# DeltaNet layer: modulation bias on VectorE and later in a round, scores on swapped PSUM banks, a later pause before the inverse's first block product

## The chip, the cores and the metric

The kernel runs on one core of a Trainium2 chip. The metric is the device time of one execution in microseconds (us). Before the change it was run three times: 2856.79 us (the median), 2857.01 and 2852.32 us. The profiled execution, from which all rows below come, took 2853.54 us, and its span is 2851.8 us.

## The reference, cut to what matters

The program is a trunk of two layers on a sequence of 1024 tokens with 1024 channels. Layer 0 mixes with a gated DeltaNet, layer 1 with stick-breaking attention, and each mixer is followed by a SwiGLU feed-forward part. Every sub-layer has a norm whose shift, scale and gate are modulations: six vectors of 1024 per layer, computed as `silu(c) @ ada_w + ada_b`. The change lies in the DeltaNet layer, which covers roughly the first 700 us:

```
G = cumsum(g);  decay = exp(G_i - G_j) where i >= j               # chunks of 64 tokens
A = where(i > j, (beta*k) k^T * decay, 0)                         # strictly lower, 64x64
U = solve(I + A, beta*v);   W = solve(I + A, beta*k*exp(G))       # the "inverse"
attn = q k^T * decay                                              # needs the scores q k^T
S' = S*exp(G_last) + k_tail^T (U - W S);  o = q_dec S + attn (U - W S)   # scan over 16 chunks
out = (rms_norm(o) * silu(z)) @ w_out                             # z: the gate's projection
```

There are 8 heads of dimension 128; the kernel takes one head per round.

## The kernel before, in words

`deltanet()` is a software pipeline over heads. In round t (`for t in range(-2, NH - 1)`, line 1246) five Python generators are merged: `stage_d(t-1)` (gates a finished head: the transposes L1235), `stage_c(t)` (the scan over chunks L1188 to L1203, and at its end the matmuls of the gate's projection z), `stage_b(t+1)` (scores, inverse, W and U of the next head), `stage_a(t+2)` (projections, convolution and norms of the head after that) and three or four modulations. After the merge, `logs()` runs the logarithms and exponentials of the norms (L977 to L991), for which ScalarE loads two tables.

`merge` (line 75) is a planner by a virtual time: each generator has a clock, starts at a head value from a list (`hd`), and each `yield x` moves its clock on by x; the one with the lowest clock issues next. The framework then schedules the instructions of each engine in one fixed order from these priorities, and inserts the semaphore waits. So a number at a `yield` or a head changes where instructions stand in all engines' queues, not how long a thing takes.

Matmul results go to PSUM banks of three pools: `big()` (tile name g, the large projections), `bank()` (name m, a ring of two banks) and `bank2()` (name s, a ring of two). `bank_swap()` takes them in turn by a counter that all its callers share: s on odd counts, m on even ones. A bank is free again when its reader, on ScalarE or VectorE, is done.

The names that the prediction uses:
- The scores are two groups of 128x64 matmuls per round, issued through `together` (whose matmuls carry the helper's lines L101 and L97), evicted by L1036 and its neighbours. The ax product (128x64 stationary, 64 moving columns) comes next.
- The inverse of I + A is made in steps. VectorE solves 16x16 blocks (L1062, L1064: `pr`, `X`), L1067 copies on ScalarE, L1069 transposes, L1072 writes the operands `dd`. Then come the block products of 32 matmuls of 64x64 each: **dd0** = `blocks(ao, d2[:, 0])` with the copy L1094, then three iterations in the loop behind it: **dd1**, **it1** and **it2**, evicted by L1100 (dd1, it1) and L1104 (it2, in two halves). Then a copy by identity (**ident**, L1112), L1108, a product S,S (L1116), a product S (L1124), and the W and U matmuls **L1133/L1137**.
- L887 transposes q, k and v of the next head, four at a time, evicted by the copies L888 on ScalarE.
- The gate: ScalarE's tanh L1148 reads all of the z projection, VectorE's L1149 multiplies. L898 and L899 are the same pair for the convolved projection.
- A modulation by rows is 8 matmuls of 32 stationary columns on an `ada` tile (`mod_rows`), a copy L200 to `adac`, one matmul L205 against a vector, and the bias addition L207.
- "gemm" below is a 128x512 matmul of a projection (L269, L271, L273; each weight is split into a high part by L263 on ScalarE and a low part by L264 on VectorE).

Of the kernel before, what the change touches and what calls it, by code (L numbers as in the profile page):

```python
# [12 lines left out]
AF = mybir.ActivationFunctionType  # L13
# [5 lines left out]
P = 128  # L19
# [12 lines left out]
def tile_trunk(ctx: ExitStack, tc: tile.TileContext, x_in, c_in, ada_w, ada_b, n1g, n2g, dn_w, dn_ab,  # L32
# [3 lines left out]
    V, S, G, PE, SY = nc.vector, nc.scalar, nc.gpsimd, nc.tensor, nc.sync  # L36
# [12 lines left out]
    def nm(s):  # L49
        uid[0] += 1  # L50
        return f"{s}_{uid[0]}"
# [7 lines left out]
    def bank(shape=(P, HALF)):  # L59
        return pm.tile(list(shape), F32, tag="m", name=nm("m"))  # L60

    def bank2(shape=(P, HALF)):
        return pq.tile(list(shape), F32, tag="s", name=nm("s"))
# [7 lines left out]
    def bank_swap(shape=(P, HALF)):  # L71
        alt[0] += 1
        return bank2(shape) if alt[0] % 2 else bank(shape)

    def merge(gens, totals=None, heads=None):

        live = [[heads[i] if heads else 0.0, i, g] for i, g in enumerate(gens)]
        rate = [1.0 / t for t in totals] if totals else [1.0] * len(gens)
        while live:
            live.sort(key=lambda e: (e[0], e[1]))  # L80
            e = live[0]
            try:
                e[0] += next(e[2]) * rate[e[1]]
            except StopIteration:
                live.remove(e)
# [5 lines left out]
    def together(made):  # L91

        last = None
        for n, f in enumerate(made):
            if n:
                with tc.high_priority():
                    ins = f()  # L97
                tc.add_manual_dep(ins.ins, last.ins.name, mybir.DependencyInfo(
                    mybir.DependencyClass.NoSync, mybir.DependencyReason.DATA), reason="together")
            else:  # L100
                ins = f()  # L101
            last = ins
# [5 lines left out]
    def const(name, shape, dt=F32):  # L108
        return cp.tile(list(shape), dt, tag=name, name=name)
# [28 lines left out]
    adab = scz[:, KT:].rearrange("p (a b) -> p a b", a=2)  # L138
# [15 lines left out]
    mod = const("mod", (P, 2, 48))  # L154

    def mod_add(ps, layer, j):
        V.tensor_tensor(out=mod[:, layer, j:j + 1], in0=ps, in1=adab[:, layer, j:j + 1], op=ALU.add)
# [45 lines left out]
    def mod_end(layer, j, acc, rows=False):  # L203
        ps = bank()
        PE.matmul(ps[:, 0:1], lhsT=acc, rhs=pick if rows else one1, start=True, stop=True)  # L205
        if rows:
            S.activation(out=mod[:, layer, j:j + 1], in_=ps[:, 0:1], func=AF.Identity, bias=adab[:, layer, j:j + 1])  # L207
        else:
            mod_add(ps[:, 0:1], layer, j)

    def first_mods(layer, q):

# [18 lines left out]
    def mod_steps(layer, js, aside=True, spare=False):  # L231
        last = None
        for j in js:
            acc = mod_unit(layer, j, aside, spare)
            if last:
                mod_end(layer, *last)
            last = (j, acc)
            yield 15.0
        mod_end(layer, *last)

    def row_steps(layer, js):
        for j in js:
            acc = mod_rows(layer, j)
            yield 15.0
            mod_end(layer, j, acc, True)
# [443 lines left out]
    def deltanet(h, after, there, second):  # L689
# [283 lines left out]
        def logs():  # L973

            pin = tc.keep_in_program_order if 1 else (lambda x: x)
            for rc, ln, bs, ot, rs in open_c:
                pin(S.activation(out=rc, in_=rc, func=AF.Ln, scale=1.0 / (P * P), bias=eps1))  # L977
            for hh, ln in open_a:
                pin(S.activation(out=ln[:, 0:2, :], in_=ln[:, 0:2, :], func=AF.Ln, bias=eps1))
            for rc, ln, bs, ot, rs in open_c:  # L980
                pin(S.activation(out=rc, in_=rc, func=AF.Exp, scale=-0.5))
                V.tensor_tensor(out=rc, in0=rc, in1=ln[:, 4, bs], op=ALU.mult)
                V.tensor_tensor(out=ot[:, bs], in0=ot[:, bs], in1=rs[:, bs].to_broadcast((P, bs.stop - bs.start, P)),
                                op=ALU.mult)
            for hh, ln in open_a:
                pin(S.activation(out=ln[:, 2:4, :], in_=ln[:, 0:2, :], func=AF.Exp, scale=-1.0))
                S.activation(out=ln[:, 4, :], in_=ln[:, 0, :], func=AF.Exp, scale=-0.5)
                S.activation(out=ln[:, 5, :], in_=ln[:, 1, :], func=AF.Exp, scale=0.5)
                V.tensor_tensor(out=ln[:, 6, :], in0=tpair[:, hh, :], in1=ln[:, 3, :], op=ALU.mult)
                V.tensor_tensor(out=ln[0:64, 8, :], in0=side[0:64, hh, :], in1=ln[0:64, 3, :], op=ALU.mult)  # L990
                V.tensor_tensor(out=ln[:, 7, :], in0=bcol[:, hh, :], in1=ln[:, 5, :], op=ALU.mult)  # L991
            open_a.clear()
            open_c.clear()

        def stage_b(hh):
# [30 lines left out]
            H = [slice(0, 64), slice(64, 128)]  # L1026
            qn = qk.rearrange("p a (n t) -> p a n t", t=P)
            for b in range(2):
                ps = bank((P, 4, 2, 64))
                together([partial(PE.matmul, ps[H[p], n, :, :], lhsT=qn[:, 1, 4 * b + n, H[p]],  # L1030
                                  rhs=qn[:, :, 4 * b + n, H[p]], start=True, stop=True)
                          for n in range(4) for p in range(2)])
                bs = slice(4 * b, 4 * b + 4)
                V.tensor_tensor(out=a1[:, bs], in0=ps[:, :, 1, :], in1=e[:, 1, bs], op=ALU.mult)
                for p in range(2):
                    V.tensor_tensor(out=at[H[p], bs, H[p]], in0=ps[H[p], :, 0, :], in1=e[H[p], 0, bs], op=ALU.mult)  # L1036
                yield 1.2

            ps = bank(C8)
# [40 lines left out]
            rg = slot("X2", (P, 2, KT, P))  # L1080
            rt, tg = rg[:, 0], rg[:, 1]
            cur0 = tg.rearrange("p n t -> p (n t)")[:, 0:KT * 64].rearrange("p (n t) -> p n t", t=64)
            yield 2.88

            def blocks(lt, rh, to=(0, 1)):

                ps = bank(C8)
                together([partial(PE.matmul, ps[H[o], n, :], lhsT=lt[H[p], n, :], rhs=rh[H[p], n, :], start=True, stop=True)
                          for n in range(KT) for p, o in (to if isinstance(to[0], tuple) else [(p, p) for p in to])])
                return ps  # L1090

            ps = blocks(ao, d2[:, 0])
# [4 lines left out]
            for it in range(3):  # L1097
                ps = blocks(nt, cur)
# [10 lines left out]
            ps = bank(C8)  # L1109
# [3 lines left out]
            ps = bank(C8)  # L1113
# [7 lines left out]
            ps = bank(C8)  # L1121
# [7 lines left out]
            for b in range(2):  # L1129
                bs = slice(4 * b, 4 * b + 4)  # L1130
                ps = bank2((P, 4, P))
# [3 lines left out]
                ps = bank((P, 4, P))  # L1135
# [32 lines left out]
        def gate_last():  # L1168
            last.append(big())
            yield 10.0  # L1170
            yield from gate_gemm(NH - 1, last[0])
# [68 lines left out]
        def stage_d(hh):  # L1240
            ot, sz = st_c.pop(hh)
            yield 3.6
            for b in range(2):
                turn_gate(ot, sz, b)
                yield 0.9
            SY.dma_start(out=yd[hh], in_=sz)

        mg = row_steps(0, range(16, 48))
        for t in range(-2, NH - 1):
            gens, hd = [], []  # L1250

            def add(g, k):
                gens.append(g)
                hd.append({'oC': 0.111, 'oM': 0.202}.get(k, 0.0))

            if t >= 1:
                add(stage_d(t - 1), 'oD')
            if t >= 0:
                add(stage_c(t), 'oC')
            if 0 <= t + 1:  # L1260
                add(stage_b(t + 1), 'oB')
            if t == -2:
                add(decays(), 'oX')
            if t + 2 < NH:
                add(stage_a(t + 2), 'oA')
            else:
                add(gate_last(), 'oA')
            add(islice(mg, (3, 3, 4, 4, 4, 4, 4, 3, 3)[t + 2]), 'oM')
            merge(gens, None, hd)
            logs()  # L1270
# [310 lines left out]
    rows = []  # L1581
# [100 lines left out]
```

## Time and profile before

| | |
|---|---|
| median of three runs | 2856.79 us |
| profiled execution, own time | 2853.54 us |
| its span | 2851.8 us |
| TensorE (PE) busy | 2726.1 us (96%) |
| VectorE (DVE) busy | 2019.9 us (71%) |
| ScalarE (ACT) busy | 1384.8 us (49%) |
| chain that ended last | PE 74%, DVE 11%, ACT 8%, DMA 3% |

A busy TensorE covers a matmul from its issue to its modelled end, so that the durations of neighbours overlap; how fast the engine works through a list is read from the starts. Idle time in brackets is the time in which an engine had nothing to run just before an instruction, with the instruction whose end released it. DeltaNet's rounds repeat: dd0 starts at 153.43, 220.43, 294.52, 371.43, 448.37, 525.22, 602.10 and 668.15 us, and L1137 at 175.71, 242.65, 319.85, 396.75, 473.69, 550.50, 628.18 and 688.10 us.

### The profile page before, as it was taken

What the parts mean: (1) busy time and instruction counts of PE and PEld (TensorE: products, weight loads), DVE (VectorE), ACT (ScalarE), POOL (GpSimd) and SP (SyncE); (2) the same over time, 40 slices, a digit from 0 to 9 for tenths busy, and PEclk for the clock granted to TensorE, in tenths of its full rate; (3) what the DMA queues carried; (4) which work ended last, traced back from release to release, by engine and by line L of the source; (5) the groups of instructions that cost most, each with busy time, mean ns of one, the idle gap of its engine ahead of it and who ended that gap; (6) DMA issues with size and microseconds to landing.
All of it is one profiled execution on the core that took longest, in us unless ns stands there. A gap on an engine that the chain in (4) does not pass through costs nothing.

```text
span 2851.8 us, 40133 instructions
## 1 busy us (share of the span) xinstructions
PE 2726.1 (96%) x15122; PEld 2171.4 (76%) x15122; DVE 2019.9 (71%) x3319; ACT 1384.8 (49%) x2924; POOL 132.8 (5%) x238
## 2 busy tenths in 40 slices
PE   6899999998999999999989999999899999999999
PEld 3677777777778887888877677677577888888887
DVE  5777666666597667667786777777868876667666
ACT  5545555554463334343245777777846332223222
POOL 0000000001000111111000000000000000000000
PEclk8999999998999999999999999999899999999999
DMA  6312222234222222222231111111412211111122
GB/s 228 106 54 82 79 72 80 72 107 133 71 85 66 68 82 71 81 75 78 67 118 52 53 52 52 53 53 50 139 52 93 61 54 57 48 56 48 56 59 100
DMA packets 139169, 218.41 MB, mean 77 GB/s; under 512 B 34016, under 2 KB 62560, under 8 KB 138976
## 3 DMA queue, kind: packets, MB, share of 16 engines
q1 hardware_dynamic: 138976, 215.86, 23.9%
q8 instruction: 119, 1.95, 0.3%
q14 instruction: 74, 0.61, 0.1%
HBM read 199.95 MB, written 15.86 MB: 76 GB/s over the span
## 4 chain that ended last, share of the span: by engine, by line
PE 74%; DVE 11%; ACT 8%; DMA 3%; issue 2%; POOL 1%; SPq 0%; ACTq 0%; POOLq 0%; DVEq 0%
PE m L269 10%; PE m L273 9%; PE m L271 9%; PE g L273 6%; PE g L269 6%; PE s L269 6%; PE s L273 6%; PE g L271 6%; PE s L271 6%; DVE S L1476 2%; PE m L97 2%; DMA ada<-in_ada_w_dram 1%; PE s L1489 1%; PE s L97 1%; PE m L101 1%
## 5 line engine op out<-in xcount | busy, mean ns | idle before, releaser
L269 PE MATMUL m<-h,wh 128*128 128x512 f32 x872 | 351.3, 411 | 12.1 <-ACT h L361 8.0
L269 PE MATMUL g<-h,wh 128*128 128x512 f32 x920 | 337.3, 405 | 10.9 <-ACT wh L263 5.8
L273 PE MATMUL m<-h,wl 128*128 128x512 f32 x872 | 341.4, 401 | 2.3 <-DVE wl L264 2.3
L273 PE MATMUL g<-h,wl 128*128 128x512 f32 x920 | 333.2, 400 | 9.1 <-DVE wl L264 9.0
L271 PE MATMUL m<-h,wh 128*128 128x512 f32 x872 | 341.1, 400 | 0.1
L271 PE MATMUL g<-h,wh 128*128 128x512 f32 x920 | 328.0, 397 | 0.0
L374 DVE SCALAR_TENSOR_TENSOR X<-m,mod,X 128x512 f32<-128x512 f32 x224 | 166.7, 749 | 202.0 <-PE m L273 201.6
L263 ACT CAST wh<-ga 128x512 fp32r<-128x512 f32 x160 | 95.7, 621 | 285.7 <-PE s L271 148.2
L273 PEld LDWEIGHTS g<-h,wl 128*128 128x128 f32 x920 | 171.9, 189 | 50.1 <-DVE wl L264 15.0
L269 PEld LDWEIGHTS m<-h,wh 128*128 128x128 f32 x872 | 167.6, 193 | 54.9 <-ACT h L361 9.8
L269 PEld LDWEIGHTS g<-h,wh 128*128 128x128 f32 x920 | 169.4, 190 | 49.1 <-ACT wh L263 10.5
L263 ACT CAST wh<-wr 128x512 fp32r<-128x512 f32 x202 | 124.7, 622 | 153.9 <-PE m L271 75.5
L271 PEld LDWEIGHTS g<-h,wh 128*128 128x128 f32 x920 | 172.1, 190 | 35.1 <-DVE h L349 0.5
L273 PEld LDWEIGHTS m<-h,wl 128*128 128x128 f32 x872 | 168.2, 193 | 39.6 <-DVE wl L264 3.1
L271 PEld LDWEIGHTS m<-h,wh 128*128 128x128 f32 x872 | 167.8, 192 | 32.9 <-DVE h L362 1.8
L1476 DVE TENSOR_TENSOR_SCAN S<-S,late 128x256 f32<-128x256 f32 (+7 forms) x128 | 171.4, 1358 | 24.3 <-ACT S L1471 24.3
L264 DVE TENSOR_TENSOR wl<-wr,wh 128x512 fp32r<-128x512 f32 x202 | 137.2, 684 | 42.0 <-ACT wh L263 41.9
L1471 ACT ACTIVATE S<-g,rq 128x512 f32<-128x512 f32 (+5 forms) x258 | 140.3, 591 | 27.7 <-DVE X L1478 9.4
L374 DVE SCALAR_TENSOR_TENSOR X<-s,mod,X 128x512 f32<-128x512 f32 x192 | 142.7, 743 | 13.2 <-PE s L273 13.0
L269 PE MATMUL m<-S,wh 128*128 128x512 f32 x352 | 138.5, 393 | 0.0
L273 PE MATMUL m<-S,wl 128*128 128x512 f32 x352 | 137.4, 390 | 0.8 <-DVE wl L264 0.8
L269 PE MATMUL s<-S,wh 128*128 128x512 f32 x352 | 137.3, 390 | 0.9 <-DVE X L374 0.9
(458 smaller groups left out, 5978.7 us busy)
## 6 DMA issues: line engine op xcount, KB each, us to landing
ada<-in_ada_w_dram SPq DMA_DIRECT2D x160, 256.0 KB, 2.6
wo<-in_ffn_wo_dram SPq DMA_DIRECT2D x96, 256.0 KB, 2.8
ga<-in_ffn_wi_dram SPq DMA_DIRECT2D x40, 512.0 KB, 3.6
ua<-in_ffn_wi_dram SPq DMA_DIRECT2D x80, 256.0 KB, 2.6
wr<-in_dn_w_dram SPq DMA_DIRECT2D x68, 256.0 KB, 2.9
wr<-in_sb_w_dram SPq DMA_DIRECT2D x54, 256.0 KB, 2.6
E<-in_ada_w_dram SPq DMA_DIRECT2D x8, 1024.0 KB, 12.0
wr<-in_ffn_wi_dram SPq DMA_DIRECT2D x32, 256.0 KB, 2.6
```

Of the source, the lines that this page charges most:

```text
L97: ins = f()
L101: ins = f()
L263: S.copy(out=hi[:, :w], in_=raw[:, :w])
L264: V.tensor_tensor(out=lo[:, :w], in0=raw[:, :w], in1=hi[:, :w].bitcast(F32), op=ALU.subtract)
L269: PE.matmul(o, lhsT=wh, rhs=mh, start=start, stop=False)
L271: PE.matmul(o, lhsT=wh, rhs=ml, start=False, stop=False)
L273: PE.matmul(o, lhsT=wl, rhs=mh, start=False, stop=stop)
L374: V.scalar_tensor_tensor(out=xs[k][:, cs], in0=ps, scalar=mod[:, layer, 24 * which + 16 + k:24 * which + 17 + k], in1=xs[k][:, cs], op0=AL ...
L1471: S.activation(out=o[hd][:, tk], in_=z[:, hd, 0:wb], func=AF.Sigmoid, scale=rq[:, c, i, hd:hd + 1])
L1476: V.tensor_tensor_scan(pw[:, 0:w][:, ::-1], pw[:, 0:w][:, ::-1], late[:, T - w:T][:, ::-1], 1.0, op0=ALU.mult, op1=ALU.max)
L1489: PE.transpose(ps[:, j, :], sgs[hd][:, (b0 + j) * P:(b0 + j + 1) * P], ident)
```

## The change

The bias of every modulation by rows is added by `mod_add` (L157, a VectorE addition that reads PSUM) in place of ScalarE's L207; there are 32 of them. The modulations' generator starts with a head of 5.0 in place of 0.202. The scores' banks come from `bank_swap` in place of `bank`. The pause ahead of dd0 in `stage_b` is 4.5 in place of 2.88.

```
     def mod_end(layer, j, acc, rows=False):
         ps = bank()
         PE.matmul(ps[:, 0:1], lhsT=acc, rhs=pick if rows else one1, start=True, stop=True)
-        if rows:
-            S.activation(out=mod[:, layer, j:j + 1], in_=ps[:, 0:1], func=AF.Identity, bias=adab[:, layer, j:j + 1])
-        else:
-            mod_add(ps[:, 0:1], layer, j)
+        mod_add(ps[:, 0:1], layer, j)
...
             for b in range(2):
-                ps = bank((P, 4, 2, 64))
+                ps = bank_swap((P, 4, 2, 64))
...
             cur0 = tg.rearrange("p n t -> p (n t)")[:, 0:KT * 64].rearrange("p (n t) -> p n t", t=64)
-            yield 2.88
+            yield 4.5
...
             def add(g, k):
                 gens.append(g)
-                hd.append({'oC': 0.111, 'oM': 0.202}.get(k, 0.0))
+                hd.append({'oC': 0.111, 'oM': 5.0}.get(k, 0.0))
```

Lines behind 206 have numbers lower by 3 in the changed kernel: L1100 becomes L1097, L1104 L1101, L1149 L1146, L887 L884, L264 L261. L157 is ahead of the edit and keeps its number.

**TensorE from it1 on, in the round whose dd0 starts at 294.52 us.** `m` and `g` are PSUM banks by pool with a running number; `X_450,S_367` are the operands of it1 and it2. Before, it1 and eleven rows behind it (it2 comes fourteen rows behind these):

```order
L101 MATMUL m_2826<-X_450_2681,S_367_2289 64x64
L97 MATMUL m_2826<-X_450_2681,S_367_2289 64x64 x15
L887 MATMUL m_2844<-ident,E_369_2292 128x128 x4
L273 MATMUL g_2316<-h_312,wl_2873 128x512
L273 MATMUL g_2316<-h_328,wl_2873 128x512
L269 MATMUL g_2316<-h_313,wh_2872 128x512
L269 MATMUL g_2316<-h_329,wh_2872 128x512
L887 MATMUL m_2850<-ident,E_369_2292 128x128 x4
L271 MATMUL g_2316<-h_321,wh_2872 128x512
L271 MATMUL g_2316<-h_337,wh_2872 128x512
L273 MATMUL g_2316<-h_313,wl_2873 128x512
L273 MATMUL g_2316<-h_329,wl_2873 128x512
```

The changed kernel, from the last gemm of the same z projection (`g_2316`) to ident:

```order
L270 MATMUL g_2316<-h_331,wl_2837 128x512
L101 MATMUL m_2877<-X_450_2681,S_367_2289 64x64
L97 MATMUL m_2877<-X_450_2681,S_367_2289 64x64 x15
L205 MATMUL m_2895<-cT,adac_2624 128x1
L101 MATMUL m_2898<-ada_2899,sc_c 32x128
L97 MATMUL m_2898<-ada_2899,sc_c 32x128 x3
L97 MATMUL m_2898<-ada_2901,sc_c 32x128 x4
L884 MATMUL m_2913<-ident,X_370_2293 128x128 x4
L884 MATMUL m_2919<-ident,X_370_2293 128x128 x4
L101 MATMUL m_2925<-X_450_2681,S_367_2289 64x64
L97 MATMUL m_2925<-X_450_2681,S_367_2289 64x64 x15
L101 MATMUL m_2946<-ident,X_450_2681 64x64
```

Before, twenty gemms and eight transposes stood between it1 and it2; now a modulation and eight transposes stand there, and no gemm. dd0 stands eight gemms earlier in the round than before, and 64 gemms follow it up to L1137 instead of 59, so that 128 instead of 133 follow from there to the next dd0.

**VectorE in the same stretch.** `X_450<-m_2826,dd` is L1100's eviction of it1 before, `X_450<-m_2877,dd` that of the changed kernel (L1097):

```order
L896 SCALAR_TENSOR_TENSOR X_370_2293<-g_2656,cw,X_370_2293 128x1022
L1100 TENSOR_TENSOR X_450_2681<-m_2826,dd 128x512
L896 SCALAR_TENSOR_TENSOR X_370_2293<-g_2656,cw,X_370_2293 128x1021
L264 TENSOR_TENSOR wl_3078<-wr_3075,wh_3077 128x512
L899 SCALAR_TENSOR_TENSOR X_370_2293<-X_370_2293 128x1024
L1149 SCALAR_TENSOR_TENSOR S_377_2315<-S_377_2315,g_2316 128x1024
L1104 TENSOR_TENSOR X_450_2681<-m_2913,dd 64x8x64 x2
L1108 TENSOR_TENSOR S_367_2289<-X_450_2681,side 64x512
```

And the changed kernel:

```order
L893 SCALAR_TENSOR_TENSOR X_370_2293<-g_2656,cw,X_370_2293 128x1021
L896 SCALAR_TENSOR_TENSOR X_370_2293<-X_370_2293 128x1024
L1146 SCALAR_TENSOR_TENSOR S_377_2315<-S_377_2315,g_2316 128x1024
L1097 TENSOR_TENSOR X_450_2681<-m_2877,dd 128x512
L157 TENSOR_TENSOR mod<-m_2895,sc_c 128x1
L1101 TENSOR_TENSOR X_450_2681<-m_2925,dd 64x8x64 x2
L261 TENSOR_TENSOR wl_3078<-wr_3075,wh_3077 128x512
L1105 TENSOR_TENSOR S_367_2289<-X_450_2681,side 64x512
```

The eviction of it1 stood four places ahead of the gate's multiplication (L1149); now it stands right behind it.

**TensorE at the scores of the next head (`E_369`).** Before, rows around the two scores:

```order
L97 MATMUL m_3105<-ada_3108,sc_c 32x128 x4
L101 MATMUL m_3125<-E_369_2292 64x128
L97 MATMUL m_3125<-E_369_2292 64x128 x7
L1235 MATMUL s_3149<-ident,E_82_425 128x128 x4
L101 MATMUL m_3155<-E_369_2292 64x128
L97 MATMUL m_3155<-E_369_2292 64x128 x7
L1195 MATMUL s_3167<-vn_3123,X_242_1529 128x128
```

And the changed kernel:

```order
L101 MATMUL s_3107<-E_369_2292 64x128
L97 MATMUL s_3107<-E_369_2292 64x128 x7
L1199 MATMUL s_3102<-vn_3105,S_365_2278 128x128
L266 MATMUL g_3074<-h_312,wh_3200 128x512
L1232 MATMUL m_3131<-ident,E_82_425 128x128 x4
L101 MATMUL s_3137<-E_369_2292 64x128
L97 MATMUL s_3137<-E_369_2292 64x128 x7
L1232 MATMUL m_3155<-ident,E_82_425 128x128 x4
```

The counter of `bank_swap` is shared with the gate's transposes (L1235, now L1232). In this round both scores take s banks and both groups of transposes take m banks, and no modulation stands ahead of the scores any more.

## Rows read from the trace of the kernel before

**Rows 1.** The page, part 1: busy time, share of the span, instructions of each engine.

```profile
PE 2726.1 (96%) x15122; PEld 2171.4 (76%) x15122; DVE 2019.9 (71%) x3319; ACT 1384.8 (49%) x2924; POOL 132.8 (5%) x238
```

**Rows 2.** Stretches: us; busy us of PE, PEld, DVE, ACT, POOL; PEclk; DMA.

```profile
294.52:319.85 25.33, 25.33 (x276) 20.57 (x277) 12.38 (x16) 12.88 (x46) 1.26 (x2) 1.00 0.19 58
319.85:371.43 51.58, 49.24 (x352) 39.99 (x351) 41.75 (x88) 26.20 (x73) 0.52 (x1) 1.00 0.29 88
118.00:120.00 2.00, 2.00 (x22) 1.35 (x24) 1.91 (x6) 0.00 (x0) 0.00 (x0) 0.50 0.81 253
668.15:688.10 19.95, 15.25 (x195) 13.62 (x195) 9.56 (x15) 10.87 (x36) 3.65 (x6) 0.50 0.46 146
```

**Rows 3.** TensorE's waits from 143 to 642 us: total us, times, longest.

```profile
PE m L101 <- ACT mod L207: 6.5, 7, 1.1
PE m L101 <- DVE dd L1072: 6.0, 7, 1.3
PE m L101 <- DVE S L1036: 2.8, 5, 0.6
```

**Rows 4.** The timeline, VectorE to dd0: start, us, instruction, [idle before <-releaser].

```profile
329.00 0.17 DVE L982 TENSOR_TENSOR rs<-rs,ln 128x8 f32<-128x8 f32 x1 [2.65 <-ACT rs L981]
...
352.62 0.35 DVE L1200 SCALAR_TENSOR_TENSOR st<-st,gl,s 128x128 f32<-128x128 f32 x1 [0.35 <-PE s L1195]
...
363.94 0.69 DVE L264 TENSOR_TENSOR wl<-wr,wh 128x512 fp32r<-128x512 f32 x1 [0.38 <-ACT wh L263]
...
368.03 1.25 DVE L1069 STREAM_TRANSPOSE S<-X 128x1024 f32<-128x1024 f32 x1 [0.94 <-ACT X L1067]
```

**Rows 5.** The timeline, TensorE from it1 on, and a modulation's last eight matmuls.

```profile
304.06 1.03 PE L97 MATMUL m<-X,S 64*64 64x64 f32 x29
305.03 0.66 PE L887 MATMUL m<-ident,E 128*128 128x128 f32 x4
305.44 0.71 PE L273 MATMUL g<-h,wl 128*128 128x512 f32 x2
...
308.28 0.62 PE L271 MATMUL g<-h,wh 128*128 128x512 f32 x2
308.75 0.62 PE L273 MATMUL g<-h,wl 128*128 128x512 f32 x2
...
328.16 0.43 PE L97 MATMUL m<-ada,sc_c 128*32 128x128 f32 x8
```

**Rows 6.** The timeline, ScalarE: the gate's tanh, one L888, one L200.

```profile
310.77 1.02 ACT L1148 ACTIVATE S<-g 128x1024 f32<-128x1024 f32 x1
312.81 0.59 ACT L888 COPY E<-m 128x512 f32<-128x512 f32 x1 [1.02 <-PE m L887]
...
325.37 0.27 ACT L200 COPY adac<-m 128x128 f32<-128x128 f32 x1
```

**Rows 7.** The timeline, VectorE: the evictions of it1 and it2, the gate's multiplication.

```profile
305.68 0.68 DVE L1100 TENSOR_TENSOR X<-m,dd 128x512 f32<-128x512 f32 x1
...
311.92 1.21 DVE L1149 SCALAR_TENSOR_TENSOR S<-S,g 128x1024 f32<-128x1024 f32 x1
313.05 1.38 DVE L1104 TENSOR_TENSOR X<-m,dd 64x512 f32<-64x512 f32 x2
```

**Rows 8.** The timeline, TensorE: one early wait, and the last head's dd0, it2, ident.

```profile
117.77 1.19 PE L269 MATMUL g<-h,wh 128*128 128x512 f32 x2 [2.02 <-ACT wh L263]
...
668.15 0.34 PE L101 MATMUL m<-dd,S 64*64 64x64 f32 x1 [3.65 <-DVE dd L1072]
...
677.50 0.34 PE L101 MATMUL m<-X,S 64*64 64x64 f32 x1 [0.89 <-DVE X L1100]
...
680.25 0.47 PE L101 MATMUL m<-ident,X 64*64 64x64 f32 x2 [0.78 <-DVE X L1104]
```

**Rows 9.** Groups by line: the bias addition on either engine (busy us, mean ns | idle before).

```profile
L207 ACT ACTIVATE mod<-m,sc_c 128x1 f32<-128x1 f32 x25 | 6.5, 260 | 22.8 <-PE m L205 22.8
L157 DVE TENSOR_TENSOR mod<-m,sc_c 128x1 f32<-128x1 f32 x48 | 7.3, 151 | 34.9 <-PE m L205 34.8
```

## The prediction

> **What bounds the kernel now.** I read the page's busy shares first, then cut DeltaNet's rounds into stretches, then read who waits for whom in TensorE's queue, and last the timelines of the places where the order changes.
>
> TensorE is busy 96% of the span [rows 1], which suggests that each of its waits costs its length. The stretches say otherwise. A steady round lasts 76.91 us, from one dd0 to the next, in two parts [rows 2]. Part (a), dd0 to L1137, lasts 25.33 us, and TensorE is busy in all of it: its matmuls set the length, and VectorE has only 12.38 us of work. Part (b), L1137 to the next dd0, lasts 51.58 us; TensorE is busy 49.24 of them and VectorE 41.75. So TensorE's 2.34 us of idle time all lie in (b), and the waits name them [rows 3]: 0.9 on average before the scores, for L207 (it frees the m bank), 0.6 before ax, for L1036, and 0.9 before dd0, for L1072.
>
> What ends last in (b) is VectorE. L1137 starts at 319.85, and VectorE waits until 329.00 for the norms' logarithms (L981), since ScalarE loads two tables for them. From 329.00 to dd0 at 371.43, whose operands it writes last, it idles only 0.35, 0.38 and 0.94 us [rows 4]. The first two of TensorE's waits therefore lie beside a VectorE queue that ends after them: without them the third one gets longer. The loop is: (a) at TensorE's pace, then 9.15 us of ScalarE's latency, then 42.4 us at VectorE's.
>
> **The change part by part.** Steady rounds first (the three from 294.52, 371.43 and 448.37), per round.
>
> *The later pause and the modulations' head, in (a).* By the order, and against what a longer pause suggests, dd0 comes eight gemms earlier, and 64 instead of 59 gemms stand in (a). Pairs of gemms start 0.47 us apart [rows 5], so five take 5 x 0.235 = +1.2 us in a stretch that TensorE sets.
>
> The larger part is the gap from it1 to ident. it1, it2 and ident depend on each other through VectorE. Before, twenty gemms and four transposes stood between it1 and it2 besides the four right behind it1, some 5.5 us of work (20 x 0.235 and twice 0.41). Now the z projection ends just ahead of it1, and a modulation and eight transposes are left. I follow the queue from it1's start, T:
> - z's last gemm ends about T + 0.1; ScalarE's tanh takes 1.02 [rows 6], to T + 1.1; VectorE's multiplication 1.21 [rows 7], to T + 2.3.
> - Only then, by VectorE's order, comes the eviction of it1, 0.68 [rows 7], to T + 3.0. It frees the m bank of the modulation, whose eight matmuls take 0.43 [rows 5], to T + 3.5.
> - L200's copy, 0.27 [rows 6], frees the bank for the second four transposes: T + 3.9. The copy L888 of the first four, 0.59 [rows 6], frees it2's bank: T + 4.6.
> - it2 takes 1.1 [rows 5], to T + 5.7, and ident follows when L1104's first half is done; in the last head, where nothing lay between, that took 0.78 more [rows 8]: T + 6.5.
>
> TensorE's own work in that time is 1.1 (it1), some 0.15 (L205, an estimate from the size of its neighbours), 0.43, twice 0.41 (the transposes, from one start to the next) [rows 5] and 1.1 (it2): 3.6 us. The rest, 2.9, is new idle time in a part that had none. Bounds: 2.0 if the tanh and the multiplication run 0.9 us earlier than I put them, 4.0 if the copies on ScalarE queue behind one another. I take +3.0.
>
> *The bias on VectorE, in (b).* L207 leaves ScalarE's queue ahead of the table loads: its 0.26 us [rows 9], of which some 0.2 before the next start. On VectorE the addition takes 0.15 [rows 9]; the order puts three per round into its dense stretch: at most +0.5. VectorE runs in order, and behind an L157 that waits for its L205 stand the solve (L1062, L1064) and, in (a), it2's eviction, for which TensorE waits. Where such additions stand elsewhere in this kernel VectorE idled 34.9 us ahead of 48, 0.73 each [rows 9], at times when it had nothing else; three of these would be +2.2 per round. In (b) it comes to them late, with the matmul long done, and I take 0.1 each.
>
> *What else (b) gives back.* The order moves two L264 to where VectorE idled 0.38 and 0.94 us [rows 4], so most of its 1.67 us of idle time is filled: −1.3. With −0.2 and +0.3 from above this would be −1.2; I take −1.0. Bounds: −1.9, all idle time and L207 gone; +2.2, nothing filled and the waits of L157 at the price above.
>
> *The scores' banks.* They end the wait for L207 before the scores and part of that for L1036, 9.3 us in 143 to 642 [rows 3]. I cost them at nothing: with five gemms less, TensorE has 48.0 us of work in a (b) of 50.6, so 2.6 us of waiting stay covered by VectorE's queue. If the cover goes, they are worth about 1.3 us a round. In steady rounds the scores don't alternate: the counter is shared, and both fall on s, where the scan's matmuls also wait.
>
> Net of a steady round: +1.2 + 3.0 − 1.0 = +3.2, and three times +9.6.
>
> *The other rounds.* Up to 294.52: twice (b) at −1.0, the first (a) four gemms shorter (−0.9), the second nine shorter with the new gap (−2.1 + 3.0), together −2.0. The round from 525.22: +4.2 in (a), and three L264 of 0.69 [rows 4] leave its (b), which with −1.0 makes +1.1. The round from 602.10: dd0 comes 21 gemms earlier, and 77 instead of 60 stand in (a): +4.0, +3.0 and −1.0, +6.0; its 3.65 us wait at the next dd0 [rows 8] is VectorE's and stays. In the last head a modulation moves into the 0.89 us wait at it2 [rows 8]: −0.9. Behind DeltaNet the order is that of before.
>
> Sum: −2.0 + 9.6 + 1.1 + 6.0 − 0.9 = +13.8. The profiled execution took 2853.54 us, 3.25 below the median of the three; from it I get 2867.3, and say **2867 us**. Own range: six gaps at 2 to 4 us (−6, +6) and seven (b) at −1.9 to +2.2, where I don't expect the bounds in all rounds at once (half of −6, +22): 2858 to 2879.
>
> **Rivals.**
>
> *B, the waits simply go (faster).* If (b) is at TensorE's pace after all, its 2.34 us of idle time end in each of seven rounds, and the gap is made up by the shorter (b): 7 x 2.34 = 16, so 2837. For it speaks the 96% [rows 1] and that 15.3 us of waits [rows 3] have their releaser moved away. Against it: dd0 itself waits for L1072 in every round, so (b) ends with VectorE.
>
> *C, nothing in sum.* VectorE is idle for half of (a) [rows 2]; were the 4.2 us that (a) gains used by it for work that now stands in (b), (b) would shrink as much as (a) grows: 2854. Against it: VectorE's order gives the same work to (b) but for what I counted, and (b) starts with ScalarE's logarithms, which wait for the end of (a). But errors of 3 us a round in my reading of the gap would give the same.
>
> *D, the clock falls in the gap (slower still).* At 117.77 TensorE had waited 2.02 us [rows 8], and the granted clock in 118 to 120 was 0.50, the 1.2 GHz level [rows 2]; in the last head, with waits under 1 us between block products, it is 0.50 for all of 668.15 to 688.10 [rows 2]. The new gap has a wait of about 1.8 us behind it1, then two of 0.5 to 0.8, among matmuls of 64 columns. If the clock falls there in six rounds, it2, ident and the first gemms behind, some 3 us of work, take up to twice as long; some of this is waiting anyway, so +1.5 a round, +9: 2876. The Trainium skill has the rule (TensorE: Matmul & The Clock Gate, "A second HAM failure mode: psum-queue depth-cycling"): short idles between groups of matmuls that cycle through PSUM banks can make the clock swing between its levels. The steady rounds of before, with waits of up to 1.1 us spread over (b), don't show it: 1.00.
>
> **How the numbers follow.** The forecast, A: 0.52, for its steps are read off the fixed order and priced from rows. D 0.13. C 0.20, B 0.15, for a long sum of small terms can turn at one misread wait. A difference under 0.2%, 5.7 us, can't be told from none. A and D are slower but for 0.02 of A; C is the same, and I leave it 0.02 of slower: faster 0.15, same 0.22, slower 0.63. The range of 8 in 10 runs from C's lower side, 2848, to D's upper side, 2881; B and the far ends stay outside.
>
> **What would show it.** In the changed profile: a wait of about 2 us behind it1 with L1097 as its releaser, and (a) of 29 to 30 us; no wait before the scores; dd0 still waiting for L1069 of the solve (the old L1072) in steady rounds, and (b) of 50 to 51 us; the round from 602.10 longer by about 6; the clock at 1.00 or, by D, below it in (a). If dd0 no longer waits for VectorE, or (a) stays under 27 us, the forecast is wrong.

## The result: slower by 0.9%

The changed kernel took 2882.21 us (median of four runs, 2875.60 to 2891.47), the kernel before 2856.28 us beside it. The ratio is 1.0093, with a 95% interval of 1.0080 to 1.0106. The forecast had the sign and most of the mechanism, and a size that was too small: 2867, with a range up to 2881. The profiled execution took 2884.37 us, its span is 2882.7.

Page, part 1, of the changed kernel, against [rows 1]:

```profile
PE 2736.4 (95%) x15122; PEld 2182.0 (76%) x15122; DVE 2025.6 (70%) x3351; ACT 1382.1 (48%) x2892; POOL 133.8 (5%) x238
```

TensorE is busy for 10 us more with the same 15122 instructions, so some of them ran slower. Three stretches (length, busy us of PE, PEld, DVE, ACT and POOL, then the clock): (a) of the first steady round, its (b), and three microseconds inside (a), against [rows 2]:

```profile
300.95:331.64 30.69, 28.23 (x280) 23.16 (x281) 12.61 (x17) 13.17 (x45) 1.26 (x2) 0.94 0.15 49
331.64:382.68 51.04, 48.08 (x348) 39.52 (x346) 42.47 (x91) 25.98 (x70) 0.52 (x1) 1.00 0.28 88
320.00:323.00 3.00, 3.00 (x34) 2.29 (x26) 0.00 (x0) 1.25 (x3) 0.00 (x0) 0.50 0.50 170
```

(a) went from 25.33 to 30.69 us, (b) from 51.58 to 51.04. (a) now holds 2.46 us of idle time where it had none, and the clock, 1.00 in every steady round before, falls to 0.50 (1.2 GHz) inside it. Where it happens, on TensorE from it1 on (start, us, instruction, [idle before <-releaser]), against [rows 5]:

```profile
316.82 1.03 PE L97 MATMUL m<-X,S 64*64 64x64 f32 x29
317.78 0.38 PE L205 MATMUL m<-cT,adac 128*128 128x1 f32 x2
319.75 0.30 PE L101 MATMUL m<-ada,sc_c 128*32 128x128 f32 x1 [1.58 <-DVE X L1097]
...
320.60 1.97 PE L884 MATMUL m<-ident,X 128*128 128x128 f32 x8
...
322.66 1.37 PE L97 MATMUL m<-X,S 64*64 64x64 f32 x29
324.91 0.29 PE L101 MATMUL m<-ident,X 64*64 64x64 f32 x2 [0.88 <-DVE X L1101]
```

And on VectorE, and ScalarE's tanh, against [rows 6, 7]:

```profile
317.87 1.22 DVE L1146 SCALAR_TENSOR_TENSOR S<-S,g 128x1024 f32<-128x1024 f32 x1 [0.95 <-ACT S L1145]
319.01 0.68 DVE L1097 TENSOR_TENSOR X<-m,dd 128x512 f32<-128x512 f32 x1
319.61 0.15 DVE L157 TENSOR_TENSOR mod<-m,sc_c 128x1 f32<-128x1 f32 x1
```

```profile
316.81 1.02 ACT L1145 ACTIVATE S<-g 128x1024 f32<-128x1024 f32 x1 [1.16 <-PE g L270]
```

That is the queue that the prediction followed, within 0.1 us up to the modulation: tanh from z's last gemm, multiplication, and only then the eviction of it1, with T = 316.71 and the modulation at T + 3.04. Behind it the transposes take 1.97 us for eight; they ran at half clock, and ident starts at T + 8.20, where the prediction had T + 6.5.

The same wait, 1.58 us for L1097, stands in six rounds, but the clock falls behind it in four of them only: those from 300.95, 382.68, 464.34 and 546.00, where ident starts at T + 8.0 to 8.2. In the round from 226.81 it stays at 1.00, and ident starts at T + 6.97 (T = 236.15):

```profile
226.81:249.82 23.01, 20.34 (x250) 16.42 (x251) 12.25 (x16) 12.70 (x45) 1.26 (x2) 1.00 0.21 64
```

```profile
239.19 0.30 PE L101 MATMUL m<-ada,sc_c 128*32 128x128 f32 x1 [1.58 <-DVE X L1097]
...
239.76 1.11 PE L884 MATMUL m<-ident,X 128*128 128x128 f32 x8
```

In the round from 626.43 the clock falls elsewhere, right behind dd0, ahead of which TensorE had waited 1.11 us; around the gap it is 1.00, with ident again at T + 6.97:

```profile
626.43:631.00 4.57, 4.57 (x40) 3.78 (x41) 3.08 (x5) 2.64 (x15) 0.00 (x0) 0.63 0.57 143
646.00:656.00 10.00, 6.52 (x112) 5.28 (x111) 4.57 (x8) 3.47 (x6) 0.00 (x0) 1.00 0.45 154
```

Within this one kernel, then, the same gap ends 1.1 to 1.3 us later where the clock fell behind the wait.

TensorE's waits from 143 to 672 us (total, times, longest), against [rows 3]:

```profile
PE m L101 <- DVE X L1097: 7.9, 5, 1.6
PE s L1185 <- DVE st L1197: 6.5, 12, 0.7
PE s L101 <- ACT E L1200: 5.9, 6, 1.1
PE m L101 <- DVE X L1101: 5.3, 6, 0.9
PE m L101 <- DVE dd L1069: 4.7, 7, 1.1
```

The wait for the bias before the scores is gone, and another stands there: the scores on s wait for the scan's copy L1200, 5.9 us in six rounds, where the bias had cost 6.5 in seven. dd0 waits for VectorE as before.

### The profile page after: what moved, and what is told of

It reads as the page before. It is cut to its first block, busy times and chain, and to the rows that moved or that the text cites. A ratio compares the mean times of both kernels' runs of the same rounds, so it can differ in the third digit from the quotient of the medians.

```text
span 2882.7 us, 40127 instructions
## 1 busy us (share of the span) xinstructions
PE 2736.4 (95%) x15122; PEld 2182.0 (76%) x15122; DVE 2025.6 (70%) x3351; ACT 1382.1 (48%) x2892; POOL 133.8 (5%) x238
## 4 chain that ended last, share of the span: by engine, by line
PE 74%; DVE 13%; ACT 8%; DMA 2%; issue 2%; POOL 1%; SPq 0%; ACTq 0%; POOLq 0%; DVEq 0%
PE m L266 10%; PE m L270 9%; PE m L268 9%; PE g L270 6%; PE g L268 6%; PE g L266 6%; PE s L266 6%; PE s L270 6%; PE s L268 6%; DVE S L1473 2%; PE m L97 2%; DMA ada<-in_ada_w_dram 2%; PE s L1486 1%; PE s L97 1%; PE m L101 1%
## 5 line engine op out<-in xcount | busy, mean ns | idle before, releaser
L260 ACT CAST wh<-ga 128x512 fp32r<-128x512 f32 x160 | 95.6, 620 | 285.7 <-PE s L268 147.7
L260 ACT CAST wh<-wr 128x512 fp32r<-128x512 f32 x202 | 124.6, 621 | 180.9 <-PE m L268 76.0
L261 DVE TENSOR_TENSOR wl<-wr,wh 128x512 fp32r<-128x512 f32 x202 | 137.3, 684 | 28.0 <-ACT wh L260 27.4
```

Of the source, the lines that this page charges most:

```text
L260: S.copy(out=hi[:, :w], in_=raw[:, :w])
L261: V.tensor_tensor(out=lo[:, :w], in0=raw[:, :w], in1=hi[:, :w].bitcast(F32), op=ALU.subtract)
```

## The experiments

Each kernel was timed against the kernel before on the same chip. (a) and (b), the waits and the clock are those of the three steady rounds, and "gemms" are those between dd0 and L1137 in TensorE's order. Two theories stood against each other at first: H, that the head alone opens the gap, and P, that the longer pause does; V blames the bias and the banks.

| kernel | gemms in (a) | waits in (a), us | clock in (a) | (a), us | (b), us | median, us |
|---|---|---|---|---|---|---|
| before | 59 | 0 | 1.00 | 25.3 | 51.6 | 2856 to 2858 |
| all four edits | 64 | 2.46 | 0.94 | 30.7 | 51.0 | 2882.2 |
| without the head | 71 | 0 to 0.1 | 1.00 | 28.5 to 28.9 | 50.5 to 51.4 | 2871.2 |
| without the pause | 55 | 3.5 | 0.94 | 29.3 | 52.7 | 2894.1 |
| head alone | 58 | 1.85 | 1.00 | 27.1 | 51.0 | 2874.1 |
| pause alone | 63 | 0 to 0.16 | 1.00 | 26.8 to 27.1 | 51.6 | 2867.8 |
| all, eviction first | 64 | 1.6 to 1.7 | 1.00 | 28.3 to 28.5 | 51.0 | 2869.2 |
| all, gap filled, 12 | 64 | 1.1 to 1.9 | 1.00 | 30.5 to 31.4 | 51.0 to 52.3 | 2884.5 |
| all, gap filled, 6 | 64 | 1.2 to 1.3 | 1.00 | 29.4 to 29.6 | 51.0 | 2877.5 |
| bias alone | 59 | 0 | 1.00 | 24.9 to 25.0 | 51.5 to 51.6 | 2854.9 |
| banks alone | 61 | 0 | 1.00 | 25.7 to 25.8 | 51.4 to 51.9 | 2857.5 |
| bias and banks | 63 | 0 to 0.1 | 1.00 | 25.8 to 26.0 | 50.4 to 50.5 | 2855.6 |

**Without the head.**

```
-                hd.append({'oC': 0.111, 'oM': 5.0}.get(k, 0.0))
+                hd.append({'oC': 0.111, 'oM': 0.202}.get(k, 0.0))
```

> The change without its head: the modulations start at 0.202 again; bias on VectorE, swapped banks and the pause of 4.5 stay. Theory H (the head brings the z projection's end ahead of the inverse's products and the modulation behind them, so that the evictions stand uncovered behind the gate's multiplication): six gemms, eight transposes and four more gemms stand between it1 and it2 again, so no wait over 0.5 us there, (a) at TensorE's pace, clock 1.00 in (a), time 2850 to 2862. Rival P (the longer pause is to blame, which puts it1's eviction behind the gate's multiplication with or without the head): a wait for L1097 of 1 us or more in each round, 2870 to 2885. Rival V (the bias on VectorE and the banks are to blame, by new waits in (b)): 2870 to 2885 with (a) clean.

2871.16 us, ratio 1.0052 (1.0035 to 1.0069). The (b) of the first steady round, then (a) and (b) of the second:

```profile
329.04:379.58 50.54, 47.05 (x341) 37.95 (x339) 42.23 (x91) 25.91 (x70) 0.52 (x1) 1.00 0.30 90
379.58:408.12 28.54, 28.54 (x288) 22.98 (x289) 12.54 (x18) 12.70 (x45) 1.27 (x2) 1.00 0.16 52
408.12:459.48 51.36, 48.41 (x340) 39.40 (x339) 42.21 (x91) 25.80 (x70) 0.52 (x1) 0.97 0.29 88
```

H was right on the gap, which is gone with the clock's fall in (a), and wrong on the time, by 9 us and more: twelve gemms came into (a), which is 3.2 us longer, and (b) gives little of it back. At a clock of 1.00 it is 1.0 us shorter than before, for some 2.8 us of gemms less (12 x 0.235). In the second and third steady round and in the one behind them the clock falls in (b), behind a wait of 1.37 to 1.40 us for L1200 at the scores, and (b) lasts 51.1 to 52.0. The time lies in P's and V's ranges as well: P's wait for L1097 is not there, and V is settled by the bias and the banks alone, further down.

**Without the pause.**

```
-            yield 4.5
+            yield 2.88
```

> The change without its pause: 2.88 again; bias on VectorE, swapped banks and the head of 5.0 stay. Theory H: now the modulation and eight transposes stand between it2 and ident, z's last gemm just ahead of it2, and L1101 behind the gate's multiplication: a gap of 2 to 4 us in each steady round, a clock under 1.00 in (a), 2870 to 2890. Rival P: 2850 to 2862, no gap. Rival V: 2870 to 2885 without a gap in (a).

2894.07 us, ratio 1.0138 (1.0119 to 1.0157): the slowest of all, 4 us above what H said. The gap stands where H put it, ahead of the modulation behind it2 (the releaser is not in the trace), and a second wait for ScalarE follows:

```profile
406.89 0.27 PE L101 MATMUL m<-ada,sc_c 128*32 128x128 f32 x1 [2.33 <-issue]
...
411.62 0.49 PE L266 MATMUL g<-h,wh 128*128 128x512 f32 x1 [0.93 <-ACT wh L260]
```

The clock falls only behind both, and stays low for longer than in the changed kernel, into (b):

```profile
410.00:412.00 2.00, 1.07 (x13) 0.74 (x11) 1.08 (x2) 1.17 (x2) 0.52 (x1) 1.00 0.07 27
412.00:414.00 2.00, 2.00 (x18) 1.84 (x18) 0.29 (x1) 0.17 (x1) 0.00 (x0) 0.58 0.29 96
414.00:415.60 1.60, 1.60 (x5) 1.21 (x6) 1.09 (x1) 0.41 (x1) 0.00 (x0) 0.50 0.16 54
415.60:418.00 2.40, 2.40 (x13) 2.40 (x12) 0.14 (x1) 0.46 (x1) 0.00 (x0) 0.50 0.00 0
418.00:421.00 3.00, 3.00 (x24) 3.00 (x24) 0.00 (x0) 2.68 (x8) 0.00 (x0) 0.81 0.00 0
```

From 412 to 421 TensorE is busy throughout, at 0.50 for most of it. L1134 to dd0 then lasts 52.66 us: VectorE's L979, behind the logarithms, starts 10.5 us into (b), where it had been 9.2. With the head in place the later pause therefore saves time, 12 us (2882 against 2894).

**The head alone** (the diff of the change's last part, on the kernel before).

> The kernel before with the head of 5.0 alone. Theory H: the gap stands between it2 and ident as in the change without its pause, 2 to 4 us a round, the m banks freed by L207 and L1104, clock under 1.00 in (a): 2868 to 2890. Rivals P and V: 2850 to 2860.

2874.11 us, ratio 1.0060 (1.0040 to 1.0080). H's time and gap are met, its clock isn't:

```profile
383.45:410.53 27.08, 25.23 (x274) 20.72 (x275) 12.52 (x17) 13.29 (x46) 1.26 (x2) 1.00 0.17 55
410.53:461.51 50.98, 49.42 (x353) 40.46 (x352) 42.01 (x88) 26.59 (x73) 0.52 (x1) 1.00 0.28 88
```

1.85 us of waits in four pieces of 0.35 to 0.68 us leave the clock at 1.00. A steady round costs 1.1 us more here, and by the profile the stretch from the first dd0 to the last L1137 is 7 us longer. This profile is 24 us above that of before; of the rest, 7 stand ahead of the first dd0 and 10 behind the last L1137, in a stretch that lasts between 2156 and 2174 us in the twelve profiles. Where those 17 come from stays open.

**The pause alone** (the third part of the change's diff, on the kernel before).

> The kernel before with the pause of 4.5 alone. Theory H: it1's eviction stands behind the gate's multiplication, but two gemms, four transposes, four gemms and four transposes stand between it1 and it2, 2.2 us of work besides it1's own 1.1, so a wait of 0 to 0.8 us a round and a clock of 1.00 in (a): 2852 to 2864. Rival P: 2868 to 2885. Rival V: 2850 to 2860.

2867.77 us, ratio 1.0045 (1.0029 to 1.0062), 4 us above H's range and at the lower end of P's.

```profile
380.56:407.65 27.09, 26.93 (x279) 21.44 (x280) 12.46 (x17) 12.98 (x46) 1.27 (x2) 1.00 0.17 54
407.65:459.28 51.63, 48.40 (x348) 39.25 (x346) 41.80 (x88) 26.22 (x73) 0.52 (x1) 1.00 0.29 88
```

There is no gap, so it isn't P's wait that costs, yet (a) is 1.5 to 1.8 longer: four gemms of 0.235 are 0.9 of it, the rest is not resolved. (b) lost those four gemms and lasts 51.63 against 51.62 us before. So H, with the head as the only cause, falls. What it lacked is the rule of the two parts itself: whatever comes into (a) is paid, and what leaves (b) is not repaid: VectorE's three waits in this (b) are still 0.35, 0.38 and 0.94 us, as in [rows 4].

**The eviction first.** The gate's multiplication is held behind the eviction of it1; TensorE's and ScalarE's orders stay those of the changed kernel.

```
+            m = V.scalar_tensor_tensor(out=sz, in0=sz, scalar=1.0, in1=zf, op0=ALU.add, op1=ALU.mult)
+            if ev[0] is not None:
+                tc.add_manual_dep(m.ins, ev[0].ins.name, mybir.DependencyInfo(
+                    mybir.DependencyClass.NoSync, mybir.DependencyReason.DATA), reason="behind")
...
+                head_norm(ot, ln, slice(0, KT))
+                yield 4.0
                 gate(zp.rearrange("p a b -> p (a b)"), sz)
-                head_norm(ot, ln, slice(0, KT))
...
+                    ev[0] = V.tensor_tensor(out=cur0, in0=ps, in1=d2[:, 1], op=ALU.add)
```

> The changed kernel with the gate's multiplication held behind it1's eviction on VectorE, in the six rounds where it stood ahead; TensorE's and ScalarE's orders are those of the changed kernel to the row. Theory H (wait behind VectorE's order, and the clock that falls in it): the wait for L1097 falls from 1.58 to about 0.4 us, the clock in (a) rises from 0.94 to 1.00, (a) from 30.7 to about 27.8 us, time 2862 to 2869. If the clock falls whatever the wait's length: (a) about 29.5, 2873 to 2878. Rival (the eviction's place doesn't matter, for the later steps of the chain wait as long): 2880 to 2885.

2869.23 us, ratio 1.0042 (1.0028 to 1.0056): 13.0 us of the 25.9 are gone. By the two traces only this multiplication changed its place on any engine, in seven rounds: in the six with the gap it now stands two places later in VectorE's queue, behind the eviction and the addition L157.

```profile
393.45 1.03 PE L97 MATMUL m<-X,S 64*64 64x64 f32 x29
...
395.28 0.30 PE L101 MATMUL m<-ada,sc_c 128*32 128x128 f32 x1 [0.48 <-DVE mod L157]
...
395.85 1.11 PE L884 MATMUL m<-ident,X 128*128 128x128 f32 x8
397.18 0.27 PE L101 MATMUL m<-X,S 64*64 64x64 f32 x1 [0.21 <-ACT E L885]
...
399.21 0.30 PE L101 MATMUL m<-ident,X 64*64 64x64 f32 x2 [0.88 <-DVE X L1101]
```

```profile
377.62:405.92 28.30, 26.72 (x281) 21.95 (x281) 12.67 (x18) 13.03 (x45) 1.27 (x2) 1.00 0.17 53
```

The first wait falls from 1.58 to 0.48, the clock stays at 1.00, and the eight transposes take 1.11 instead of 1.97 us. ident starts at T + 5.87 in all six rounds, 1.1 us earlier than where the clock had stayed up. (a) loses 2.0 to 2.4 us in the four rounds in which the clock had fallen behind the wait, 1.1 in the round from 226.81, and 3.7 in that from 626.43, where the fall behind dd0 and a wait for L260 are gone too. That is 13.7 in sum, for the 13.0 that was measured.

**The gap filled.** To part the clock from the wait, unread matmuls go into the gap.

```
+        fill = 12 if rows and j in (23, 27, 31, 35, 39, 43, 46) else 0
+        together([partial(PE.matmul, ps[:, 0:1], lhsT=acc, rhs=pick if rows else one1, start=True, stop=True)]
+                 + [partial(PE.matmul, ps[:, P:2 * P], lhsT=acc, rhs=ident, start=True, stop=True) for _ in range(fill)])
```

> The changed kernel with twelve matmuls of 128x128 whose result nothing reads behind L205 in the gap of each of seven rounds, some 1.5 us of work where TensorE waited 1.58; all orders are otherwise those of the changed kernel. Theory H with the clock as a price of its own: the clock in (a) stays at 1.00, the modulation, the eight transposes and it2 behind the gap take 2.4 instead of 4.1 us, (a) about 29 us, time 2869 to 2877. Rival W (the waits alone cost, and the fallen clock hides in other waits): no change, 2880 to 2886. If the clock falls all the same: 2880 to 2886 with the clock under 1.00.

2884.53 us, ratio 1.0094 (1.0070 to 1.0119). The time speaks for W, the trace for H, so this run did not decide: the clock was 1.00 in (a), but each of the twelve counts as two matmuls in the trace, they took 2.92 us, and what the clock gave back they cost: ident starts at T + 8.11. In two rounds (b) is longer besides (52.2 and 52.3 us), with VectorE waiting 1.06 and 1.25 us for a weight's copy (L262). With `fill = 6`:

> The changed kernel with six of the unread matmuls of 128x128 behind L205 in the gap instead of twelve: the twelve took 2.92 us where 1.58 were free, so that they pushed the modulation back by about 0.9 while the clock stayed at 1.00; six should take 1.46 and push nothing. Theory H with the clock as a price of its own: clock 1.00 in (a), the modulation's matmuls start as far behind it1 as in the changed kernel (3.0 us), (a) 29.0 to 29.4 instead of 30.7, time 2870 to 2878. Rival W (the clock's fall costs nothing of its own): (a) 30.4 or more, 2880 to 2886.

2877.53 us, ratio 1.0077 (1.0046 to 1.0108).

```profile
396.99 1.03 PE L97 MATMUL m<-X,S 64*64 64x64 f32 x29
...
398.20 1.58 PE L97 MATMUL m<-ident,adac 128*128 128x128 f32 x12
399.92 0.30 PE L101 MATMUL m<-ada,sc_c 128*32 128x128 f32 x1
...
400.49 1.11 PE L886 MATMUL m<-ident,X 128*128 128x128 f32 x8
```

```profile
381.15:410.58 29.43, 28.20 (x292) 23.27 (x293) 12.84 (x18) 13.04 (x45) 1.26 (x2) 1.00 0.16 51
```

The modulation starts at T + 3.04 (T = 396.88), just as in the changed kernel, so the wait is the same, only filled, and ident starts at T + 6.97 in all six rounds. (a) is 29.4 to 29.6 instead of 30.5 to 30.7 in the four rounds in which the clock had fallen behind the wait: the fall has a price of its own, 1.0 to 1.3 us each, and W is out. In the round from 226.72 (a) is 23.01 as in the changed kernel, where the clock had not fallen either; in that from 622.70 it fell right behind dd0, ahead of the gap, as in the changed kernel. The four rounds make 4.6 us, and the medians differ by 4.7; but the intervals of the two ratios overlap, so that the proof is (a) and not the time.

**The bias alone, the banks alone, and both** (the first and second parts of the diff, on the kernel before).

> The kernel before with the bias on VectorE alone: (a) keeps its 59 gemms and their cover of the inverse's products. Theory H: (a) 25.3 us; (b) loses L207 on ScalarE (0.2) and gains three additions on VectorE (0.3 to 0.5): time 2851 to 2859. Rival V (additions hold up VectorE's queue while they wait for their matmul): (b) longer by 1 to 2 us, 2862 to 2870. Rival B of the prediction (TensorE's wait for L207 at the scores was worth its length): 2848 or less.

2854.92 us, ratio 0.9989 (0.9977 to 1.0001).

> The kernel before with the scores on swapped banks alone: 61 instead of 59 gemms in (a), none missing between the inverse's products. Theory H with the rule that (a) is at TensorE's pace and (b) at VectorE's: (a) +0.5 us, (b) unchanged though two gemms fewer stand in it and the wait for L207 at the scores goes: 2856 to 2862. Rival B: (b) shorter by about 1 us, 2848 to 2853. Rival V (scores on s collide with the scan): (b) longer by over 1 us, 2862 to 2870.

2857.47 us, ratio 0.9998 (0.9983 to 1.0013).

> The kernel before with the bias on VectorE and the swapped banks, without pause and head: 63 gemms in (a), the inverse's products covered as before. Rule of two parts ((a) at TensorE's pace, (b) at VectorE's): (a) +0.9 over the 25.0 of the bias alone, (b) 51.4 or a little less; time 2856 to 2863, behind the bias alone. If TensorE's waits in (b) are worth their length after all: 2848 to 2853, ahead of both.

2855.62 us, ratio 0.9999 (0.9986 to 1.0012). (a) and (b), the first pair of the bias alone, the second of the banks alone, the third of both:

```profile
374.22:399.14 24.92, 24.92 (x275) 20.65 (x276) 12.77 (x18) 12.84 (x45) 1.27 (x2) 1.00 0.20 59
399.14:450.61 51.47, 49.67 (x352) 39.86 (x350) 42.14 (x91) 25.62 (x70) 0.52 (x1) 1.00 0.28 88
```

```profile
372.59:398.36 25.77, 25.77 (x277) 20.96 (x278) 12.38 (x17) 12.88 (x46) 1.26 (x2) 1.00 0.18 57
398.36:450.26 51.90, 49.35 (x350) 39.60 (x348) 42.17 (x88) 26.36 (x73) 0.52 (x1) 1.00 0.29 87
```

```profile
371.19:396.97 25.78, 25.78 (x279) 21.40 (x280) 12.77 (x18) 12.73 (x45) 1.26 (x2) 1.00 0.19 58
396.97:447.43 50.46, 48.85 (x348) 39.31 (x346) 42.25 (x91) 25.89 (x70) 0.52 (x1) 1.00 0.29 89
```

None of the three can be told from the kernel before, and V is out for the bias and the banks alone. The bias alone leaves TensorE's wait for VectorE at dd0 in place. With both, (b) is shorter by 1.2 us, more than I expected, and (a)'s four gemms take 0.5 to 0.6 of it back. VectorE's queue has the reason: behind the logarithms it had waited 1.67 us in three places [rows 4], and with both edits one wait of 0.41 is left:

```profile
427.39 0.29 DVE L1188 TENSOR_TENSOR vn<-s,E 128x128 f32<-128x128 f32 x1 [0.41 <-PE s L1186]
```

No version tried is clearly faster than the kernel before.

## Why the prediction was wrong

By its own terms, from profile to profile (span +30.9 us):

| stretch | forecast, us | measured, us |
|---|---|---|
| up to the dd0 that was at 294.52 | −2.0 | +6.4 |
| three steady rounds | +9.6 | +14.4 |
| round from 525.22 | +1.1 | +3.6 |
| round from 602.10 | +6.0 | +8.5 |
| last head, up to L1137 | −0.9 | −1.1 |
| behind it | 0 | −0.9 |

Of the 17.1 us that the sum lacks, falls of the clock make 6.2 (four in the gap and one behind dd0), the stretch ahead of the first dd0 5.9 (3.2 of them luck), and the two rounds behind that stretch 2.5.

- *What bounds the rounds*: right, and shown best by the kernels that open no gap. (a) follows its gemms to within about 1 us (24.9 to 25.3 us with 59, 25.8 to 27.1 with 63, 28.5 to 28.9 with 71), (b) stays within 50.4 to 51.9 us while TensorE's work in it changes from 47.1 to 49.7. In the second steady round of each of the twelve kernels VectorE's last write of dd0's operands ends 0.05 to 0.06 us ahead of dd0.
- *The gap from it1 to ident*: right in place and releaser; eviction first takes away 1.1 us of it, and the clock's fall with it. Its idle time is 2.46 us, where the term said 2.9 of 3.0. Where the clock stayed up, ident starts at T + 6.97, for the T + 6.5 of the sum.
- *The clock in the gap*: the step that failed. I gave it as rival D, at 0.13 and 1.5 us a round, and left it out of the sum as if it were either the gap or the clock. It came on top of the gap, at some 1.2 us in each of four rounds, 4.6 in all, and in two rounds with the same wait it did not come. The row that spoke for it was [rows 8]: a wait of 2.02 us, and the clock at 0.50 behind it. What decides whether the clock falls behind such a wait, no run here shows. Of the Trainium skill's rule on the clock (TensorE: Matmul & The Clock Gate, "A second HAM failure mode: psum-queue depth-cycling") the changed trace shows the case: waits for a PSUM bank between groups of matmuls, and a clock that falls to its lower level in (a) of four of the six rounds with the gap and rises again. The head alone, with 1.85 us in four pieces in each steady round, does not show it.
- *What (b) gives back*: −1.0 forecast, −0.5 measured. L207's 0.2 ahead of the logarithms came as forecast: VectorE goes on from them 8.97 us into (b), where it had been 9.15. From there to dd0, the changed kernel and the one before, and the two waits that are left in the changed one:

```profile
340.61:382.68 42.07, 39.88 (x278) 32.48 (x278) 40.74 (x87) 18.15 (x52) 0.52 (x1) 1.00 0.31 95
329.00:371.43 42.43, 40.51 (x265) 32.70 (x266) 40.21 (x85) 18.19 (x54) 0.52 (x1) 1.00 0.30 88
```

```profile
368.72 0.29 DVE L1188 TENSOR_TENSOR vn<-s,X 128x128 f32<-128x128 f32 x1 [0.28 <-PE s L1186]
...
378.83 1.25 DVE L1066 STREAM_TRANSPOSE S<-X 128x1024 f32<-128x1024 f32 x1 [0.38 <-ACT X L1064]
```

Here the waits fell from 1.67 to 0.66 us as forecast, but VectorE has 0.53 us more to do, partly the additions, so its stretch is only 0.36 us shorter. An addition does wait for its matmul, 2.93 us in each round, but ahead of the logarithms, where VectorE had nothing else to do. TensorE's new waits (L1185 for L1197, the scores for L1200) did not set the end of (b): dd0 still waits for VectorE.
- *The start*: −2.0 forecast, +6.4 measured. The sum put the stretch ahead of the first dd0 at nothing, without a reason, and 5.9 of the 6.4 lie there. 3.2 of them lie ahead of the first projection gemm (45.16 us, 41.94 before), where no instruction was changed; in other executions that gemm starts between 41.46 and 45.91, with either kind of kernel. So the kernel before was profiled with a quick start, which is luck, and against the medians the change costs 25.9 us and not 30.8. The other 2.7 lie between that gemm and the first dd0, in a stretch whose order I did not work through; bias and banks together show 2.6 there, and the cause stays open. The two rounds behind it cost 0.5 instead of the −2.0 of the sum: the first (a) is 0.4 longer where −0.9 was forecast, and its (b) lasts what it did.
- *The round from 602.10*: 2.5 more than forecast. A wait for L260 is 0.81 of it, and the clock's fall behind dd0 about 1.6: sixty matmuls further on, the same matmul starts 9.14 us behind dd0, and 7.56 with the eviction first, where the clock did not fall there.
- *Rivals*: B's premise, that TensorE's waits in (b) are worth their length, is not borne out: dd0 waits for VectorE in every kernel, and where (b) is shorter VectorE had waited less. (Of the 15.3 us that I counted for B only 9.3 had a releaser that the change moved away; the other 6.0 are the waits for L1072.) C did not happen, since hardly any of VectorE's work moved into (a): 12.61 us for 12.38.

## What to carry to other kernels

Cut a loop at the points where its pace changes hands and ask for each edit into which part it moves work: work that comes into the part at TensorE's pace is paid in full, and work that leaves the part at another engine's pace is repaid only as far as that engine then waits less. Where a chain of small dependent products runs through PSUM, what stands between its links on TensorE is its cover, and the place of each eviction in VectorE's queue counts as much as the bank; a gap that opens there must be priced together with the clock, not as an alternative to it, and as a chance: the same gap cost 1.2 us more in four rounds and nothing more in two. An edit that looks neutral alone can be dear beside another: the bias and the banks cost nothing alone, but 20 us with the head and without the pause (2894 against 2874).

## What the runs showed of the hardware that was not expected

- The same wait of 1.58 us among small matmuls stood in six rounds of the changed kernel. In four the granted clock fell behind it and stayed at 0.50 for about 3 us, at a price of some 1.2 us each; in two it stayed at 1.00. With 0.48, 0.21 and 0.88 us in the same place it did not fall in any of the six.
- Six matmuls whose results nobody reads, in that same wait, kept the clock at 1.00 behind it in all six rounds, and (a) was 1.0 to 1.3 us shorter in the four.
- A longer wait did not always mean a fall. Without the head the clock fell in (b) behind waits of 1.37 to 1.40 us at the scores and stayed up behind one of 1.33; with the pause alone it stayed up behind one of 1.50 and fell in another round behind one of 1.40.
- Without the pause it fell only some 5 us behind the first wait, among dense work, and 7 us of dense work ran at the lower level for the most part.
- The start of the kernel, ahead of any changed instruction, differs by up to 4.5 us between the twelve profiles.
